# Rotated queries and keys kept in DRAM as head, frequency, half, high or low

## The chip, the cores and the metric

One core of one Trainium2 chip runs the kernel. The metric is the device time of one execution in microseconds (us), and lower is better. The kernel before takes 2559.37 us, the median of three runs (2557.65 to 2565.87).

## The reference

Two decoder layers work on 1024 tokens of width 1024, in float32. Each layer has a mixer with three groups of heads side by side, and then an MLP. Cut to what matters here:

```python
def hybrid_layer(x, ...):
    z = rms_norm(x, g_pre_mix) @ w_in
    mq, mk, mv, mo, mi, mf, sq, sk, sv, dq, dk, dv = split_columns(z)
    # mLSTM: 4 heads of 64, a causal convolution on q and k, a scan over 8 chunks of 128
    h_m = mlstm_chunkwise(...)
    # sliding window attention: 8 query heads, 2 key heads of 64, window 128, sinks
    s_q, s_k = rope(sq, pos), rope(sk, pos)
    out_s = sliding_window_gqa(s_q, s_k, s_v, sinks)
    # differential attention: 4 heads, two maps each, query and key width 32, causal
    d_q, d_k = rope(dq, pos), rope(dk, pos)
    out_d = rms_norm(differential_attention(d_q, d_k, d_v, lam), sub_g) * (1 - lam_init)
    x = x + rms_norm(concat([out_m, out_s, out_d]) @ w_out, g_post_mix)
    u = square(relu(rms_norm(x, g_pre_mlp) @ w_up))
    return x + rms_norm(u @ w_down, g_post_mlp)

def rope(x, pos):          # x: (batch, seq, heads, d)
    x1, x2 = x[..., :d // 2], x[..., d // 2:]
    return concat([x1 * cos - x2 * sin, x2 * cos + x1 * sin])
```

The rotation acts on each frequency of a head: entry p of the first half and entry p of the second half are turned together. The order in which the rows of a head lie does not matter for the scores, as long as queries and keys have the same order.

## The kernel before

Matrix products are done with each float32 operand split into a high part (rounded to the matmul's format) and a low part (the rest), so that one product becomes two or three matmuls (high by high, high by low, low by high).

A layer goes through these stages. In the first layer: the gates and values (`p_g2`), the projection of the differential queries and keys (`p_d`), the differential attention (`e_diff`), the projection of the window attention's queries and keys (`p_s`), the values and output gates of the mLSTM (`p_g1`), its queries and keys (`p_m`), the window attention together with the mLSTM, the output projection, the MLP. In the second layer `p_d` comes ahead of `p_g2`, and `p_m` ahead of `p_s`. The tile scheduler orders every engine's instructions beforehand, by priorities (`ahead(n)` raises them); each engine then runs its list in that order, and the stages named above overlap: matmuls of `p_s` (line 285) stand between those of the differential attention (lines 493, 520, 528).

A projection (`proj_tiles`) gives 128 rows by 512 tokens at a time in PSUM, for each of two halves of the sequence. For the rotated operands the columns of the weights are permuted on the host, so that one projection tile holds the first halves of several heads, 16 or 32 frequencies each, and the next tile the second halves. `rope_pair` rotates a pair of such tiles on the vector engine (DVE) into two tiles `rot`, splits each with `hi_lo`, and stores the parts to scratch tensors in DRAM. `rope_single` does the same for the keys of the window attention, where both halves lie in one tile. These stores are four for a pair of tiles and half of the sequence: two tiles, high and low each. Per layer 16 go to `d_rope` (256 KB each), 16 to `s_ropeq` (256 KB) and 8 to `s_ropek` (128 KB).

The attention stages load the rows back in the layout that the matmuls want: `diff_load` (lines 446 to 466) puts the high rows of a head's keys into 32 partitions and its high and low rows into 64 more, and the queries so that high meets low; the sum over 96 partitions is then the three products at once. `swa_load` (lines 573 to 590) does so for the window attention with 128 partitions. So these loads cannot begin before the stores have landed.

Nearly all DMA instructions, stores and loads and weights (`rw`, line 109), are issued by one engine, SyncE (SP), in one order that was fixed when the kernel was built. SP waits in front of each for whatever that transfer needs. A tile `rot` shares its buffers with other tiles (tags `e` and `at`, `ws` and `pt`), so that a buffer is free again only when its store has landed; `oo` (line 556), the last tile of a differential head, goes to `mix_d` by a store on SP too and shares the buffers `od` with `ot` (line 530).

Of the kernel before, what the change touches and what calls it, by code (L numbers as in the profile page):

```python
# [10 lines left out]
F32 = mybir.dt.float32  # L11
# [7 lines left out]
T = 1024  # L19
# [15 lines left out]
def hybrid_kernel(ctx: ExitStack, tc: tile.TileContext, x_in, w_t, w_g, w_v, w_out, w_up, w_down,  # L35
                  pb, cv, gains, g_mlp, rope_t, masks, out):
    nc = tc.nc
# [31 lines left out]
    dr = ctx.enter_context(tc.tile_pool(name="dr", bufs=2, space=bass.MemoryType.DRAM))  # L69
# [3 lines left out]
    def new(tag, shape, name, dt=F32):  # L73
        return pools[tag].tile(list(shape), dt, name=name, tag=tag)
# [7 lines left out]
    def EV(name, dt=F32, shape=(P, 512)):  # L82
        return new("ev", shape, name, dt)

    def PS(tag, name):
        return new(tag, (P, 512), name)

    def ahead(n):

        return tc.high_priority(offset=n) if n else nullcontext()  # L90
# [112 lines left out]
    for j in range(4):  # L203
        if j == 1:
            load_x(1)
        r = new("wd", (P, 2, 392), "wg0")
# [11 lines left out]
    for l in range(DEPTH):  # L218
# [22 lines left out]

        d_rope = [dr.tile([8, 2, 2, 16, T], F32, name=f"d_rope{i}") for i in range(2)]
        s_ropeq = dr.tile([8, 2, 2, 32, T], F32, name="s_ropeq")
        s_ropek = dr.tile([2, 2, 2, 32, T], F32, name="s_ropek")
        m_qk = dr.tile([4, P, T], F32, name="m_qk")
        m_v = dr.tile([T, 256], F32, name="m_v")
        m_g = dr.tile([T, 256], F32, name="m_g")
# [6 lines left out]
        def proj_tiles(*groups):  # L256


            wts = []
            for idx, _, _, _, wtag in groups:  # L260
                for i in idx:
                    if wtag == "whl":
                        w = new("whl", (P, 2, 1024), "wt", F32R)
                        hi, lo = w[:, 0], w[:, 1]
                    else:
                        hi, lo = (new(wt_, (P, 1024), "wt", F32R) for wt_ in wtag)
                    load_w(hi, lo, w_t[l, i], 512)
                    wts.append((hi, lo))
            for half in range(2):
                wi = iter(wts)  # L270
                for idx, evac, tables, rtag, _ in groups:
                    if tables is not None:
                        with ahead(1000):
                            tab = new(rtag[1], (P, 2, 512), "tab")
                            nc.sync.dma_start(tab, rope_t[tables, :, :, half * 512:(half + 1) * 512])
                    qs = []
                    for i in idx:
                        hi, lo = next(wi)
                        q = PS("mm", "pt")
                        n = 0  # L280
                        for k in range(8):
                            kc = slice(k * P, (k + 1) * P)
                            for a, b in ((hi[:, kc], hT[half][:, :, kc]), (hi[:, kc], lT[half][:, :, kc]),
                                         (lo[:, kc], hT[half][:, :, kc])):
                                nc.tensor.matmul(q, lhsT=a, rhs=b, start=n == 0, stop=n == 23)  # L285
                                n += 1
                        qs.append(q)
                        if tables is None:
                            with ahead(1000):
                                evac(i, half, q)  # L290
                    if tables is not None:
                        with ahead(1000):
                            evac(half, qs, tab, rtag[0])

        def hi_lo(r, store):

            hi = r[:, 0].bitcast(F32R)
            nc.scalar.copy(hi, r[:, 1])
            store(0)
            nc.vector.tensor_sub(r[:, 1], r[:, 1], r[:, 0])  # L300
            store(1)

        def rope_pair(d, h0, nh):

            def f(half, qs, tab, tag):
                qa, qb = qs
                c, sn = tab[:, 0], tab[:, 1]
                hs = slice(half * 512, (half + 1) * 512)
                ra, rb = (new(tag, (P, 2, 512), "rot") for _ in range(2))
                t = EV("t")  # L310
                nc.vector.tensor_mul(ra[:, 1], qa, c)
                nc.vector.tensor_mul(rb[:, 1], qa, sn)
                nc.vector.tensor_mul(t, qb, sn)
                nc.vector.tensor_sub(ra[:, 1], ra[:, 1], t)
                nc.vector.tensor_mul(t, qb, c)
                nc.vector.tensor_add(rb[:, 1], rb[:, 1], t)
                for x_, r in enumerate((ra, rb)):
                    hi_lo(r, lambda s_: nc.sync.dma_start(d[h0:h0 + nh, s_, x_, :, hs], r[:, s_]))
            return f

        def rope_single(d):

            def f(half, qs, tab, tag):
                q, = qs
                c, sn = tab[:, 0], tab[:, 1]
                hs = slice(half * 512, (half + 1) * 512)
                r = new(tag, (P, 2, 512), "rot")
                t = EV("t")
                nc.vector.tensor_mul(r[:, 1], q, c)
                nc.vector.tensor_mul(t[0:64], q[64:128], sn[64:128])  # L330
                nc.vector.tensor_mul(t[64:128], q[0:64], sn[0:64])
                nc.vector.tensor_sub(r[0:64, 1], r[0:64, 1], t[0:64])
                nc.vector.tensor_add(r[64:128, 1], r[64:128, 1], t[64:128])
                def store(s_):
                    for x_ in range(2):
                        nc.sync.dma_start(d[:, s_, x_, :, hs], r[x_ * 64:(x_ + 1) * 64, s_])
                hi_lo(r, store)
            return f

# [106 lines left out]
        def diff_load(h, hf):  # L446

            ks = []
            if hf == 0:
                k_ = new("wd", (P, 2, 512), "ks", F32R)  # L450
                src = d_rope[1][2 * h:2 * h + 2, :, :, :, 0:512].rearrange("m s x p n -> (s x p) m n")
                nc.sync.dma_start(k_[0:32].bitcast(F32), src[0:32])
                nc.sync.dma_start(k_[32:96].bitcast(F32), src)
                ks = [k_[:, m] for m in range(2)]
            else:
                for m in range(2):
                    k_ = new("wd", (P, T), "ks", F32R)
                    src = d_rope[1][2 * h + m].rearrange("s x p n -> (s x p) n")
                    nc.sync.dma_start(k_[0:32].bitcast(F32), src[0:32])
                    nc.sync.dma_start(k_[32:96].bitcast(F32), src)  # L460
                    ks.append(k_)
            q_ = new("wd", (P, 2, 512), "qs", F32R)
            src = d_rope[0][2 * h:2 * h + 2, :, :, :, hf * 512:(hf + 1) * 512].rearrange("m s x p n -> (s x p) m n")
            nc.sync.dma_start(q_[0:64].bitcast(F32), src)
            nc.sync.dma_start(q_[64:96].bitcast(F32), src[0:32])
            return ks, q_

        drd = {}
# [104 lines left out]
        def swa_load(kv, hf):  # L573
            if hf == 0:
                kk = []
                for s_ in range(2):
                    k_ = new("ws", (P, T), "kk", F32R)
                    for j in range(2):
                        nc.sync.dma_start(k_[j * 64:(j + 1) * 64].bitcast(F32),
                                          s_ropek[kv, s_].rearrange("x p n -> (x p) n"))  # L580
                    kk.append(k_)
                sop["k"] = kk
            qq = []
            for pr in range(2):
                w = new("ws", (P, 2, 512), "qq", F32R)
                h0 = kv * 4 + pr * 2
                nc.sync.dma_start(w.bitcast(F32), s_ropeq[h0:h0 + 2, :, :, :, hf * 512:(hf + 1) * 512]
                                  .rearrange("m s x p n -> (s x p) m n"))
                qq.append(w)
            sop["q"] = qq  # L590

        def swa1(kv, i):
            if i % 4 == 0:
                swa_load(kv, i // 4)
# [334 lines left out]
            acc.extend(BIG3(f"acc{i}", F32) for i in range(2))  # L929

        def p_d():
            proj_tiles(((0, 1), rope_pair(d_rope[0], 0, 8), 0, ("e", "at"), "whl"),
                       ((2, 3), rope_pair(d_rope[1], 0, 8), 1, ("e", "at"), ("wd", "ws")))

        def p_g2():
# [88 lines left out]
        for c in range(len(ffs)):  # L1024
# [30 lines left out]
            def down_mm(q, t, n, f, i):  # L1055
                for a, b in ((0, 0), (0, 1), (1, 0)):
                    nc.tensor.matmul(q, lhsT=U[f][a][:, t * P:(t + 1) * P], rhs=D[f][b][:, n * 512:(n + 1) * 512],  # L1057
                                     start=i == 0, stop=i == 3 * nf - 1)
                    i += 1
                return i  # L1060
# [43 lines left out]
            for j, (t, n) in enumerate(groups[4:]):  # L1104
                q = PS(ptag[j % 4], "pd")
                i = 0
                for f in range(nf):
                    i = down_mm(q, t, n, f, i)
# [93 lines left out]
```

## Time and profile before

| what | value |
|---|---|
| median of 3 runs | 2559.37 us |
| the profiled execution, its own time | 2563.38 us |
| its span, first to last instruction | 2561.6 us |
| TensorE matmul busy | 2397.5 us (94%) |
| VectorE busy | 1457.8 us (57%) |
| ScalarE busy | 1076.1 us (42%) |
| DMA, moved in all | 227.42 MB, mean 89 GB/s |
| chain that ended last: PE, DMA, DVE | 73%, 11%, 7% |

The span stands 1.8 us below the execution's own time, and that execution stands 4.0 us above the median of the three runs. PE is TensorE, DVE is VectorE, ACT is ScalarE, POOL is GpSimd, SP is SyncE; "SPq" marks DMA issues by SP. A row of the chain of waits has the start in us, the duration in us, and what the chain went through. A row of a table of stretches has the stretch, its length, the busy us of PE, of its weight loads, of DVE, ACT and POOL with instruction counts, the clock that TensorE was granted (1.00 is full), the mean busy share of the core's 16 DMA engines, and what they moved in GB/s. A row of the timeline of SP has start, duration, line, transfer and count; where several issues are merged, the duration includes waits between them.

### The profile page before, as it was taken

To read this page: it belongs to the slowest core of one execution; us is meant where nothing else is said; L and a number is where in the kernel's file an instruction comes from. 1 tells how busy PE (TensorE), PEld (TensorE's weight loads), DVE (VectorE), ACT (ScalarE), POOL (GpSimd) and SP (SyncE) were. 2 spreads that over 40 slices of the span, in tenths; PEclk is the share of its full clock that TensorE was granted. 3 is DMA by queue.
4 is the path that set the end of the run, shared out by engine and by line. 5 is a ranking of instruction groups with operands and counts; after the bars stand their busy time and mean duration, and the time that the engine had idled before them with its cause. 6 is when DMAs were issued, how large, how long until landed. Compare 5 with 4: busy or idle time off the path is not lost.

```text
span 2561.6 us, 32491 instructions
## 1 busy us (share of the span) xinstructions
PE 2397.5 (94%) x11556; PEld 1991.8 (78%) x11556; DVE 1457.8 (57%) x3604; ACT 1076.1 (42%) x2657; POOL 90.8 (4%) x174
## 2 busy tenths in 40 slices
PE   8888989889999999999999998878899999999998
PEld 7767867667888888888778777867678888888887
DVE  6676888775234434443675876867742344334436
ACT  4244777656313312331433645756553123213312
POOL 0000000010000000000000000000100000000000
PEclk9998999999999999999999989989999999999999
DMA  5444354333012101110442334433321112112204
GB/s 169 146 141 132 92 125 121 100 103 107 25 41 66 59 24 50 66 50 25 173 163 86 117 126 132 137 87 106 113 90 41 34 58 66 32 36 66 66 22 160
DMA packets 146002, 227.42 MB, mean 89 GB/s; under 512 B 22512, under 2 KB 60592, under 8 KB 145840
## 3 DMA queue, kind: packets, MB, share of 16 engines
q1 hardware_dynamic: 143680, 221.70, 28.1%
q10 hardware_dynamic: 2160, 3.65, 0.4%
q8 instruction: 91, 1.49, 0.2%
q14 instruction: 71, 0.58, 0.1%
HBM read 179.09 MB, written 46.20 MB: 88 GB/s over the span
## 4 chain that ended last, share of the span: by engine, by line
PE 73%; DMA 11%; DVE 7%; ACT 4%; issue 2%; POOL 1%; SPq 1%; DVEq 0%; POOLq 0%; ACTq 0%
PE pu L1012 26%; PE pd L1057 25%; PE pt L285 7%; PE po L848 2%; PE pg L356 2%; PE pn L356 2%; POOL rs L153 1%; DMA mb<-m_rows 1%; DMA qs<-d_rope 1%; PE pv L528 1%; DMA mix_d<-oo 1%; PE sp L493 1%; DMA mxl<-mix_d 1%; DMA rw<-in_w_t_dram 1%; PE ss L611 1%
## 5 line engine op out<-in xcount | busy, mean ns | idle before, releaser
L1012 PE MATMUL pu<-h2T,wu 128*128 128x512 f32 x3072 | 703.6, 390 | 0.1
L1012 PEld LDWEIGHTS pu<-h2T,wu 128*128 128x128 f32 x3072 | 577.4, 188 | 121.2 <-DVE h2T L94 1.1
L1057 PE MATMUL pd<-wdh,u 128*128 128x512 f32 x2048 | 635.2, 390 | 1.1 <-DVE acm L1068 1.1
L1057 PEld LDWEIGHTS pd<-wdh,u 128*128 128x128 f32 x2048 | 384.8, 188 | 81.1 <-DVE acm L1068 1.5
L1057 PE MATMUL pd<-wdl,u 128*128 128x512 f32 x1024 | 399.0, 390 | 0.0
L1068 DVE TENSOR_TENSOR acm<-acm,pd 128x512 f32<-128x512 f32 x224 | 153.1, 686 | 309.1 <-PE pd L1057 309.0
L1015 ACT ACTIVATE r<-pu 128x512 f32<-128x512 f32 x128 | 75.2, 588 | 537.9 <-PE pu L1012 537.9
L285 PE MATMUL pt<-hT,wt 128*128 128x512 f32 x832 | 287.2, 411 | 2.7 <-DVE lamp L228 1.5
L116 ACT ACTIVATE wu<-rw,gk 128x128 fp32r<-128x128 f32 x512 | 160.2, 390 | 184.7 <-PE pu L1012 132.3
L117 DVE SCALAR_TENSOR_TENSOR wu<-rw,gk,wu 128x128 fp32r<-128x128 f32 x512 | 154.2, 351 | 140.9 <-ACT wu L116 140.8
L1057 PEld LDWEIGHTS pd<-wdl,u 128*128 128x128 f32 x1024 | 192.6, 188 | 39.8
L1018 DVE TENSOR_TENSOR r<-r 128x512 f32<-128x512 f32 x128 | 88.4, 690 | 222.5 <-ACT u L1017 222.5
L285 PEld LDWEIGHTS pt<-hT,wt 128*128 128x128 f32 x832 | 160.5, 196 | 33.6 <-issue 2.3
L285 PE MATMUL pt<-lT,wt 128*128 128x512 f32 x416 | 170.2, 409 | 0.0
L153 POOL TENSOR_TENSOR rs<-ms,mhalf 128x1 f32<-128x1 f32 (+2 forms) x112 | 78.9, 709 | 2351.8 <-DVE ms L151 2283.2
L94 DVE TENSOR_TENSOR wdl<-rw,wdh 128x512 fp32r<-128x512 f32 x128 | 88.5, 692 | 105.1 <-ACT wdh L93 105.0
L848 PE MATMUL po<-woh,mxl 128*128 128x512 f32 x384 | 135.1, 410 | 10.4 <-DVE acc L856 7.8
L93 ACT CAST wdh<-rw 128x512 fp32r<-128x512 f32 x128 | 79.3, 620 | 129.2 <-DMA rw<-in_w_down_dram 129.2
L499 ACT ACTIVATE e<-e,nb 128x256 f32<-128x256 f32 (+7 forms) x128 | 99.4, 777 | 52.4 <-DVE nb L496 47.1
L493 PE MATMUL sp<-ks,qs 96*128 96x512 f32 (+2 forms) x192 | 74.0, 396 | 41.0 <-DMA qs<-d_rope 17.0
L356 PE MATMUL pn<-wv,hT 128*128 128x256 f32 x512 | 110.0, 296 | 0.2 <-ACT mv L707 0.2
L496 DVE CUSTOM_DVE_ANT_0 e<-sp,mdif 128x512 f32<-128x512 f32 (+3 forms) x128 | 74.5, 585 | 33.1 <-PE sp L493 24.0
(225 smaller groups left out, 3361.0 us busy)
## 6 DMA issues: line engine op xcount, KB each, us to landing
rw<-in_w_up_dram SPq DMA_DIRECT2D x128, 256.0 KB
rw<-in_w_down_dram SPq DMA_DIRECT2D x128, 256.0 KB
rw<-in_w_t_dram SPq DMA_DIRECT2D x52, 256.0 KB
tab<-in_rope_dram SPq DMA_DIRECT2D x20, 512.0 KB
xt<-in_x_dram SPq DMA_DIRECT2D x16, 512.0 KB
d_rope<-rot SPq DMA_DIRECT2D x32, 256.0 KB
s_ropeq<-rot SPq DMA_DIRECT2D x32, 256.0 KB
qq<-s_ropeq SPq DMA_DIRECT2D x16, 512.0 KB
```

The costliest lines, as they stand in the source:

```text
L94: nc.vector.tensor_sub(lo, src, hi.bitcast(F32))
L116: nc.scalar.activation(hi[:, cs], rj, AF.Copy, scale=g)
L117: nc.vector.scalar_tensor_tensor(out=lo[:, cs], in0=rj, scalar=g, in1=hi[:, cs].bitcast(F32), op0=ALU.mult, op1=ALU.subtract)
L153: nc.gpsimd.tensor_tensor(out=rs, in0=ms, in1=mhalf[:, 0:n], op=ALU.pow)
L285: nc.tensor.matmul(q, lhsT=a, rhs=b, start=n == 0, stop=n == 23)
L356: nc.tensor.matmul(q[:, 0:n], lhsT=a, rhs=b, start=i == 0, stop=i == 23)
L493: nc.tensor.matmul(sp[:, 0:w], lhsT=qs[0:96, m, (q % 4) * P:(q % 4 + 1) * P], rhs=ks[m][0:96, c0:c0 + w], start=True, stop=True)
L499: nc.scalar.activation(e[:, 0:L], e[:, 0:L], AF.Exp, bias=nb[:, nch - 1:nch], scale=-1.0, accum_out=den[:, m:m + 1])
L848: nc.tensor.matmul(q, lhsT=mx[:, a, k], rhs=wo[k][b][:, n * 512:(n + 1) * 512], start=i == 0, stop=i == 3 * nk - 1)
L1012: nc.tensor.matmul(q, lhsT=w[:, a, kc], rhs=h2[b + half][:, :, kc], start=n == 0, stop=n == 23)
L1057: nc.tensor.matmul(q, lhsT=U[f][a][:, t * P:(t + 1) * P], rhs=D[f][b][:, n * 512:(n + 1) * 512], start=i == 0, stop=i == 3 * nf - 1)
L1068: nc.vector.tensor_add(a, a, q)
```

## The change

The three scratch tensors get another order of dimensions. Before, a head's block was laid out as high or low, half (`x`), frequency, token. Now it is frequency, half, high or low, token. A store takes one half and one of high or low for all heads and all frequencies; its rows on the DRAM side are now `(h p)`, 128 rows of equal spacing (64 for `s_ropek`), where they were 8 heads of 16 rows, 4 heads of 32 rows or 2 heads of 32 rows. The spacing of the 2 KB rows of one store is 16 KB now; before it was 4 KB within a head.

The loads follow. The 64 rows of a head, now in the order frequency, half, high or low, still lie next to each other. The rows of the high parts alone are every second row now. For the differential queries the roles are turned: low comes first in memory (`low_first`), the load of 32 rows brings what is stored at place 1 (the high parts), and it is issued ahead of the load of 64 rows. For the window attention's keys each load of 64 rows goes to every second partition (`k_[j::2]`), 0, 2, 4 ... or 1, 3, 5 ..., where it went to partitions 0 to 63 or 64 to 127.

```diff
-        d_rope = [dr.tile([8, 2, 2, 16, T], F32, name=f"d_rope{i}") for i in range(2)]
-        s_ropeq = dr.tile([8, 2, 2, 32, T], F32, name="s_ropeq")
-        s_ropek = dr.tile([2, 2, 2, 32, T], F32, name="s_ropek")
+        d_rope = [dr.tile([8, 16, 2, 2, T], F32, name=f"d_rope{i}") for i in range(2)]
+        s_ropeq = dr.tile([8, 32, 2, 2, T], F32, name="s_ropeq")
+        s_ropek = dr.tile([2, 32, 2, 2, T], F32, name="s_ropek")
...
-        def rope_pair(d, h0, nh):
+        def rope_pair(d, h0, nh, low_first=False):
...
-                    hi_lo(r, lambda s_: nc.sync.dma_start(d[h0:h0 + nh, s_, x_, :, hs], r[:, s_]))
+                    hi_lo(r, lambda s_: nc.sync.dma_start(
+                        d[h0:h0 + nh, :, x_, 1 - s_ if low_first else s_, hs].rearrange("h p n -> (h p) n"), r[:, s_]))
...
-                        nc.sync.dma_start(d[:, s_, x_, :, hs], r[x_ * 64:(x_ + 1) * 64, s_])
+                        nc.sync.dma_start(d[:, :, x_, s_, hs].rearrange("h p n -> (h p) n"), r[x_ * 64:(x_ + 1) * 64, s_])
...
-                src = d_rope[1][2 * h:2 * h + 2, :, :, :, 0:512].rearrange("m s x p n -> (s x p) m n")
-                nc.sync.dma_start(k_[0:32].bitcast(F32), src[0:32])
-                nc.sync.dma_start(k_[32:96].bitcast(F32), src)
+                src = d_rope[1][2 * h:2 * h + 2, :, :, :, 0:512]
+                nc.sync.dma_start(k_[0:32].bitcast(F32), src[:, :, :, 0].rearrange("m p x n -> (p x) m n"))
+                nc.sync.dma_start(k_[32:96].bitcast(F32), src.rearrange("m p x s n -> (p x s) m n"))
...
-                    src = d_rope[1][2 * h + m].rearrange("s x p n -> (s x p) n")
-                    nc.sync.dma_start(k_[0:32].bitcast(F32), src[0:32])
-                    nc.sync.dma_start(k_[32:96].bitcast(F32), src)
+                    src = d_rope[1][2 * h + m]
+                    nc.sync.dma_start(k_[0:32].bitcast(F32), src[:, :, 0].rearrange("p x n -> (p x) n"))
+                    nc.sync.dma_start(k_[32:96].bitcast(F32), src.rearrange("p x s n -> (p x s) n"))
...
-            src = d_rope[0][2 * h:2 * h + 2, :, :, :, hf * 512:(hf + 1) * 512].rearrange("m s x p n -> (s x p) m n")
-            nc.sync.dma_start(q_[0:64].bitcast(F32), src)
-            nc.sync.dma_start(q_[64:96].bitcast(F32), src[0:32])
+            src = d_rope[0][2 * h:2 * h + 2, :, :, :, hf * 512:(hf + 1) * 512]
+            nc.sync.dma_start(q_[0:32].bitcast(F32), src[:, :, :, 1].rearrange("m p x n -> (p x) m n"))
+            nc.sync.dma_start(q_[32:96].bitcast(F32), src.rearrange("m p x s n -> (p x s) m n"))
...
-                        nc.sync.dma_start(k_[j * 64:(j + 1) * 64].bitcast(F32),
-                                          s_ropek[kv, s_].rearrange("x p n -> (x p) n"))
+                        nc.sync.dma_start(k_[j::2].bitcast(F32), s_ropek[kv, :, :, s_].rearrange("p x n -> (p x) n"))
...
-                                  .rearrange("m s x p n -> (s x p) m n"))
+                                  .rearrange("m p x s n -> (p x s) m n"))
...
-            proj_tiles(((0, 1), rope_pair(d_rope[0], 0, 8), 0, ("e", "at"), "whl"),
+            proj_tiles(((0, 1), rope_pair(d_rope[0], 0, 8, True), 0, ("e", "at"), "whl"),
```

The instructions of PE, DVE, ACT and POOL stay the same and stand in the same order. On SP the order stays too, but for the two query loads of a head, of which the smaller is now the first. Two places on SP show it. The first is in the first layer, where the keys of the window attention are stored while the differential attention runs; before:

```order
L460 DMA ks<-d_rope_191 64x1024
L464 DMA qs<-d_rope_190 64x2x512
L336 DMA s_ropek<-rot 2x32x512 x4
L465 DMA qs<-d_rope_190 32x2x512
L275 DMA tab<-in_rope_dram 128x2x512
```

and now:

```order
L462 DMA ks<-d_rope_191 64x1024
L466 DMA qs<-d_rope_190 32x2x512
L338 DMA s_ropek<-rot 64x512 x4
L467 DMA qs<-d_rope_190 64x2x512
L276 DMA tab<-in_rope_dram 128x2x512
```

The four key stores stand between the two query loads of the next head (`qs`) in both; the load behind them is now the one of 64 rows (256 KB), and it was the one of 32 rows (128 KB). The second place is in the second layer, where queries of the window attention are stored; before:

```order
L318 DMA s_ropeq<-rot 4x32x512 x3
L109 DMA rw<-in_w_t_dram 128x512 x2
L464 DMA qs<-d_rope_11178 64x2x512
L465 DMA qs<-d_rope_11178 32x2x512
L459 DMA ks<-d_rope_11179 32x1024
L460 DMA ks<-d_rope_11179 64x1024
L558 DMA mix_d<-oo 64x256
```

and now:

```order
L319 DMA s_ropeq<-rot 128x512 x3
L109 DMA rw<-in_w_t_dram 128x512 x2
L466 DMA qs<-d_rope_11178 32x2x512
L467 DMA qs<-d_rope_11178 64x2x512
L461 DMA ks<-d_rope_11179 32x1024
L462 DMA ks<-d_rope_11179 64x1024
L560 DMA mix_d<-oo 64x256
```

Here nothing but the order within the pair of query loads has moved; the stores ahead of them have another shape on the DRAM side.

## The prediction

> **What bounds the kernel now.** I read the chain of waits first, then tables of stretches around each place where it runs through a DMA in the attention part, then the timeline of SP there. The change can act only where rotated tiles are stored and loaded back, in the attention part of each layer. There the chain has long DMA pieces:
>
> ```profile
> 98.99 6.41 DMA rw<-in_w_t_dram
> 126.39 11.16 DMA qs<-d_rope
> 161.59 7.86 DMA ks<-d_rope
> 194.71 3.72 issue
> 221.08 10.12 DMA mix_d<-oo
> ...
> 1341.87 5.75 DMA rw<-in_w_g_dram
> 1461.40 12.51 DMA qs<-d_rope
> 1500.91 8.68 DMA qs<-d_rope
> 1532.20 9.55 DMA mix_d<-oo
> 1562.28 8.30 DMA mix_d<-oo
> 1572.41 3.00 DMA ks<-d_rope
> ```
>
> A load of 256 KB takes 3.00 us when little stands ahead of it (last row); the others, of 64 to 256 KB, take 5.75 to 12.51. What stands ahead is seen in the table of stretches (the last two columns are the share of 16 DMA engines and GB/s):
>
> ```profile
> 133.00:139.00 6.00, 1.31 (x4) 1.25 (x5) 0.51 (x1) 0.00 (x0) 0.00 (x0) 0.70 0.13 51
> 160.00:161.00 1.00, 1.00 (x9) 0.91 (x8) 1.00 (x3) 0.09 (x1) 0.00 (x0) 1.00 0.25 96
> 112.00:116.00 4.00, 3.90 (x18) 2.92 (x17) 1.73 (x7) 1.91 (x6) 0.00 (x0) 1.00 0.52 186
> 1405.50:1406.00 0.50, 0.50 (x3) 0.38 (x2) 0.50 (x4) 0.50 (x3) 0.00 (x0) 1.00 1.03 393
> ```
>
> Behind key stores (2 heads outermost) the share is 0.13, two engines of 16, for six microseconds on end; behind the window queries' stores (4 heads) 0.25, four engines; behind the differential stores (8 heads) 0.52, eight. About 24 to 25 GB/s an engine each time. The last stretch lies behind one store of 256 KB with 128 rows (`m_qk`, alone in the queue): all engines, 393 GB/s. So the stores crowd onto as many engines as their outermost dimension has rows, and every later transfer that has a share of its bytes on those engines waits behind them.
>
> [...]
>
> SP suffers too:
>
> ```profile
> 1404.59 0.34 SPq L691 DMA_DIRECT2D m_qk<-yc  x1
> ...
> 1458.46 2.90 SPq L336 DMA_DIRECT2D s_ropek<-rot  x4
> ...
> 1467.47 8.00 SPq L336 DMA_DIRECT2D s_ropek<-rot  x4
> ```
>
> Four key stores hold SP for 2.90 us, and while earlier ones still drain, 8.00.
>
> **The change part by part.** *Stores.* Four key stores are 4 x 128 KB = 0.52 MB: 10.3 us at 51 GB/s, 1.3 at 393, 9.0 less. Four query stores of the window attention, 1.05 MB: 10.9 us at 96 GB/s, 2.7 at 393, 8.2 less. Four differential stores: 5.6 us at 186 GB/s, 2.7 after, 2.9 less. These times matter only where someone waits. Ten gaps of PE lie there, each followed by a stretch with a reduced granted clock (column before the last two):
>
> ```profile
> 102.50:107.60 5.10, 0.00 (x1) 0.00 (x0) 1.53 (x5) 0.62 (x1) 0.00 (x0) 0.71 0.32 109
> 107.60:112.00 4.40, 4.38 (x12) 3.60 (x13) 4.23 (x12) 2.12 (x7) 0.00 (x0) 0.56 0.41 111
> 132.00:137.70 5.70, 0.19 (x2) 0.05 (x1) 0.69 (x1) 0.17 (x1) 0.00 (x0) 0.79 0.13 51
> 137.70:142.00 4.30, 4.30 (x13) 3.72 (x14) 2.40 (x8) 1.59 (x7) 0.00 (x0) 0.50 0.20 63
> 164.60:169.50 4.90, 0.00 (x0) 0.03 (x1) 2.15 (x6) 1.50 (x3) 0.00 (x0) 1.00 0.49 155
> 169.50:174.00 4.50, 4.50 (x14) 3.73 (x15) 2.98 (x5) 1.72 (x3) 0.00 (x0) 0.62 0.26 87
> 194.70:198.40 3.70, 0.01 (x1) 0.00 (x1) 2.20 (x6) 2.09 (x9) 0.89 (x2) 0.78 0.61 223
> 198.40:204.00 5.60, 5.57 (x15) 4.41 (x16) 1.78 (x9) 0.05 (x1) 0.00 (x0) 0.53 0.64 209
> 228.00:235.50 7.50, 1.42 (x6) 1.04 (x5) 1.35 (x5) 2.72 (x9) 0.89 (x2) 0.69 0.80 197
> 235.50:238.00 2.50, 2.44 (x11) 2.47 (x12) 1.78 (x5) 0.49 (x2) 0.00 (x0) 0.50 0.33 128
> 1345.00:1348.60 3.60, 0.00 (x0) 0.00 (x0) 0.41 (x1) 0.94 (x2) 0.00 (x0) 0.79 0.25 87
> 1348.60:1353.00 4.40, 3.81 (x11) 3.40 (x12) 4.33 (x9) 1.14 (x2) 0.00 (x0) 0.50 0.45 103
> 1467.60:1474.00 6.40, 0.00 (x0) 0.00 (x0) 0.66 (x2) 0.92 (x4) 0.89 (x2) 0.68 0.45 158
> 1474.00:1480.00 6.00, 5.96 (x15) 4.72 (x16) 4.10 (x13) 0.00 (x0) 0.00 (x0) 0.50 0.32 107
> 1505.60:1509.80 4.20, 0.00 (x0) 0.00 (x0) 0.98 (x2) 1.56 (x5) 0.00 (x0) 0.73 0.19 69
> 1509.80:1515.00 5.20, 5.17 (x15) 4.15 (x16) 3.62 (x9) 2.71 (x5) 0.89 (x2) 0.56 0.50 144
> 1538.00:1542.80 4.80, 0.96 (x6) 0.49 (x4) 0.98 (x5) 1.34 (x6) 0.00 (x0) 0.88 0.57 199
> 1542.80:1548.00 5.20, 5.18 (x14) 4.21 (x15) 2.31 (x9) 2.31 (x7) 0.89 (x2) 0.50 0.31 80
> 1570.50:1576.00 5.50, 1.96 (x14) 1.59 (x13) 1.56 (x6) 2.46 (x8) 0.89 (x2) 0.98 0.84 191
> 1576.00:1579.00 3.00, 3.00 (x16) 2.94 (x15) 1.97 (x7) 0.62 (x3) 0.00 (x0) 0.50 0.00 0
> ```
>
> Idle time of PE in the gaps: 5.1 + 5.5 + 4.9 + 3.7 + 6.1 in the first layer, 3.6 + 6.4 + 4.2 + 3.8 + 3.5 in the second, 46.8 us. Behind each, length times missing clock: 1.9 + 2.2 + 1.7 + 2.6 + 1.3 and 2.2 + 3.0 + 2.3 + 2.6 + 1.5, 21.3 us. All of it together, 68 us, is the most that the gaps can give.
>
> Gap by gap: the second and the seventh wait for a query load behind key stores; 9.0 us less is more than the gap, and 126.39 + 3.0 or 1461.40 + 3.0 lies ahead of where PE ran dry (132.0, 1467.6). I take gap and clock: 7.7 and 9.4. The third and the eighth wait behind window query stores; 161.59 + 3.0 and 1500.91 + 3.0 are no later than 164.6 and 1505.6: 6.6 and 6.5. The first and the sixth wait for weights behind differential stores: 2.9 us each, clock not counted since a gap remains. In the other four the share is 0.57 to 0.84, so bandwidth for loads is needed there anyway, or the chain names no cause ("issue"); between nothing and all I take half of gap and clock: 3.2, 3.7, 3.2, 2.5. Sum: 24.1 + 24.5 = 48.6 us.
>
> *What comes back.* When DMA is early, DVE is late next. It did 1.5 + 0.7 + 2.2 + 2.2 + 1.4 and 0.4 + 0.7 + 1.0 + 1.0 + 1.6 = 12.5 us inside the gaps, and right behind them it has little room:
>
> ```profile
> 140.00:164.00 24.00, 23.68 (x115) 19.07 (x115) 21.36 (x56) 12.90 (x32) 0.90 (x2) 0.95 0.50 157
> ```
>
> 89% of that stretch. So of the work done in the gaps I charge the part of the gaps that goes, 48.6 of 68: 8.9 us. Net 39.7.
>
> *Loads.* Same bytes in rows of the same length. The second query load brings 128 KB more behind the key stores, 0.3 us at 393 GB/s, with 2.6 us to spare at 132.0: nothing; without that cover, 0.3 a head. Keys to every second partition is a form that the trace does not have. Its nearest row is the same load as now:
>
> ```profile
> 1688.57 9.37 DMA kk<-s_ropek
> ```
>
> Four groups of such loads run per execution. If they took twice as long, at most 4 x 9.4 = 37 us; if shorter, the same bound below nothing. I take nothing, since rows, bytes and the number of rows per load are the same.
>
> *Issue.* A store of 128 rows may cost SP 0.34 us (`m_qk`) where four key stores now cost 0.7 each at best; SP's long holds end. I count nothing: those holds are the same time as the waits above.
>
> **The rivals.** *DVE and ACT take over, the gain is small.* For it: 89% above. Then only the four gaps behind 2 and 4 engines give their idle time, 5.5 + 6.4 + 4.9 + 4.2 = 21.0, less DVE's work in them, 4.5: 16.5 us, 2543 against the median; with two of the four refilled, 8 us, 2551. Against it: in the gaps DVE and ACT mostly stand still with PE, so all are delayed alike.
>
> *No change that can be told.* The loads are late anyway: in 228.0 to 235.5 and in 1570.5 to 1576.0 the engines are 0.80 and 0.84 busy, and spread stores put bytes on engines that had been free for loads. That all ten gaps are such is against the 0.13 of the second. That the stores do not spread although they are now 128 rows (the change not doing what it says) is against the 393 GB/s of `m_qk`. Within 7.7 us of 2559.
>
> *Slower: rows 16 KB apart.* One store now writes 2 KB in every 16 KB, and if DRAM takes such a pattern badly, all 16 engines stand in a slow write and everything queues behind it. Now a layer's stores take 4 x 5.6 + 4 x 10.9 + 2 x 10.3 = 86.6 us for 9.4 MB, 109 GB/s; below that the change loses. At 51 GB/s it would be 185 us, 98 more per layer; as 68 of 173 us are on the path now, 0.39 of 197 is 77 us: 2636. For it, no store of the trace has this spacing; against it, `m_qk` writes 2 KB in every 4 KB at full rate.
>
> [...]
>
> **How the numbers follow.** Profiled execution 2563.4 - 39.7 = 2523.7; it stands 4.0 above the median, so 2519.6 for a median. The first case (16 to 68 us won, 2491 to 2543) has 0.72, more than 68 won 0.02, DVE taking over with 8 to 16 won 0.10, no change 0.10, slower 0.06. The range goes from all gaps and clocks gone, 2491, to just past the four gaps' bound, 2547, which leaves out the lower half of the small gains, no change and slower. A difference under 0.3%, 7.7 us, cannot be told from none: faster 0.84, same 0.10, slower 0.06.
>
> **What would show it.** In the profile after: stretches with a share of 0.13, 0.25 or 0.5 in the store batches give way to short ones near 1.0; the query load behind the key stores is under 4.5 us in the chain or gone from it; the gaps at the second, third, seventh and eighth place go, with the half clock behind them; four key stores hold SP under 3 us each time; DVE's share in these stages rises. It would be wrong if the gaps stay with a load or DVE named in place of the store, if stores show a high share at low GB/s (the slower rival), or if the key loads to every second partition turn up longer than 9.4 us.

## The result, and the profile after

The changed kernel takes 2483.06 us (median of 4 runs, 2480.93 to 2487.86) against 2559.03 of the kernel before: ratio 0.9701, 95% interval 0.9678 to 0.9723. That is 76 us won, where 40 were forecast. The direction and the mechanism hold; the time lies outside the range, which ended at 2491. The profiled execution has a span of 2486.1 us, 75.5 less than before.

The page of the changed kernel gives the chain of waits by engine; DMA had 11% of it before:

```profile
span 2486.1 us, 32491 instructions
PE 78%; DVE 8%; DMA 5%; ACT 4%; issue 2%; POOL 2%; SPq 0%; POOLq 0%; DVEq 0%; ACTq 0%
```

In the changed kernel the places of the former gaps read as follows, in the table of stretches (columns as before). The first four rows lie where the first, second, third and fifth gap lay in the first layer, the last three where the seventh and the eighth lay in the second:

```profile
102.00:107.00 5.00, 5.00 (x25) 4.03 (x24) 4.73 (x13) 2.31 (x7) 0.00 (x0) 1.00 0.33 107
125.00:130.00 5.00, 5.00 (x29) 4.01 (x28) 4.13 (x13) 2.37 (x8) 0.00 (x0) 1.00 0.75 206
150.00:155.00 5.00, 5.00 (x24) 4.16 (x23) 5.00 (x12) 3.42 (x6) 0.00 (x0) 1.00 0.78 261
201.50:207.00 5.50, 5.47 (x46) 5.23 (x45) 3.96 (x15) 3.52 (x11) 0.89 (x2) 1.00 0.40 131
...
1424.50:1430.00 5.50, 5.47 (x28) 4.05 (x27) 5.09 (x16) 2.44 (x7) 0.89 (x2) 1.00 0.85 267
1430.00:1436.00 6.00, 6.00 (x35) 5.02 (x34) 5.56 (x18) 3.92 (x13) 0.00 (x0) 1.00 0.05 18
1453.00:1458.00 5.00, 5.00 (x24) 4.15 (x24) 4.68 (x12) 2.48 (x4) 0.89 (x2) 1.00 0.54 163
```

PE is busy throughout these rows and the granted clock is 1.00; at the other four places it is the same. DVE is 83 to 100% busy in six of the seven rows, and it does not hold PE up. In the view of who waits for whom, from 55 to 210 us, these are all waits of PE that are left (name, what ended the wait, us in total, times, the longest); in the second layer, from 1300 to 1560, the longest is 0.7 us:

```profile
PE trd L522 <- DVE on L549: 0.6, 1, 0.6
PE sp L495 <- DVE nb L498: 0.5, 1, 0.5
PE nat L540 <- DVE on L549: 0.4, 1, 0.4
PE pt L286 <- DVE rot L313: 0.2, 1, 0.2
PE trd L522 <- ACT oo L559: 0.2, 1, 0.2
```

No DMA is left among the long pieces of the chain in either stretch. The stores land early (DMA issues of the changed kernel; the last number is the median time from issue to landing), and SP is no longer held by four key stores (timeline of SP, second layer):

```profile
d_rope<-rot SPq DMA_DIRECT2D x32, 256.0 KB, 3.2
s_ropeq<-rot SPq DMA_DIRECT2D x32, 256.0 KB, 2.7
s_ropek<-rot SPq DMA_DIRECT2D x16, 128.0 KB, 2.3
```

```profile
1415.37 2.79 SPq L338 DMA_DIRECT2D s_ropek<-rot  x4
...
1423.83 2.39 SPq L338 DMA_DIRECT2D s_ropek<-rot  x4
```

The second group held SP for 8.00 us before, and does so for 2.39 now.

Since PE's instructions are the same in the same order, every matmul of one trace can be set against the same matmul of the other. The table has, at matmuls around the ten gaps, how much earlier each runs than in the kernel before (us), for the changed kernel and for four experiments told below; worked out from the start times in the traces:

```
start before   changed   none spread   only d_rope   only s_ropek   only s_ropeq
    95.6        -1.6        -0.5           1.1           -1.5           -1.6
   118.5         6.2        -0.5           8.7           -1.7           -1.5
   142.1        13.7        -1.1           7.8            5.8           -2.4
   180.0        20.4        -0.5           7.8            5.7            4.3
   215.1        26.5        -0.2           8.0            7.2           10.4
   260.0        35.6         1.4           9.6            8.0           19.5
  1300.8        34.6         2.9           8.5           10.5           18.3
  1362.1        43.1         2.9          17.1           11.2           17.9
  1490.0        52.6         4.8          17.7           20.8           18.2
  1520.1        59.2         5.5          17.6           21.3           24.8
  1556.1        65.4         8.7          17.5           24.2           31.0
  1580.1        70.7         9.7          18.3           25.9           36.2
  1630.3        70.5         9.7          18.3           25.9           36.1
  1860.0        76.0         7.5          19.2           50.0           29.7
```

The gain comes in ten steps at the ten gaps: 7.7, 7.6, 6.7, 6.1, 9.1 in the first layer, 8.5, 9.6, 6.6, 6.2, 5.2 in the second, 73.3 us together (from unrounded differences). Ahead of the first the changed kernel is 1.6 us behind, and behind the last it wins another 4.8. Between the steps the difference hardly moves; in the whole MLP it stands still (34.4 from 600 to 1200).

Each trace is one execution, and that limits how finely the columns can be read: `none spread` rises to 9.7 although no store is spread, by up to 3 us at a gap, but its trace is 4 us under the median of its kernel and that of the kernel before 4 us above its own. A step of 2 or 3 us is not taken as an effect here.

### The profile page after: what moved, and what is told of

The parts are those of the page before. It is cut to its first block, busy times and chain, and to the rows that moved or that the text cites. A ratio compares the mean times of both kernels' runs of the same rounds, so it can differ in the third digit from the quotient of the medians.

```text
span 2486.1 us, 32491 instructions
## 1 busy us (share of the span) xinstructions
PE 2380.3 (96%) x11556; PEld 1977.1 (80%) x11556; DVE 1456.5 (59%) x3604; ACT 1074.4 (43%) x2657; POOL 91.3 (4%) x174
## 4 chain that ended last, share of the span: by engine, by line
PE 78%; DVE 8%; DMA 5%; ACT 4%; issue 2%; POOL 2%; SPq 0%; POOLq 0%; DVEq 0%; ACTq 0%
PE pu L1013 26%; PE pd L1058 26%; PE pt L286 9%; PE po L849 3%; PE pn L358 3%; PE pg L358 2%; POOL rs L153 2%; DMA mb<-m_rows 2%; PE pv L530 2%; PE sp L495 1%; PE trd L522 1%; DMA mxl<-mix_d 1%; PE ss L612 1%; ACT junk L159 1%; PE pvs L646 1%
## 5 line engine op out<-in xcount | busy, mean ns | idle before, releaser
L286 PE MATMUL pt<-hT,wt 128*128 128x512 f32 x832 | 279.5, 401 | 2.0 <-DVE lamp L228 1.5
L1058 PEld LDWEIGHTS pd<-wdl,u 128*128 128x128 f32 x1024 | 192.5, 188 | 39.9
L286 PEld LDWEIGHTS pt<-hT,wt 128*128 128x128 f32 x832 | 155.5, 190 | 31.0 <-issue 1.9
L849 PEld LDWEIGHTS po<-woh,mxl 128*128 128x128 f32 x384 | 73.3, 194 | 22.9 <-DVE acc L857 7.9
L1020 DVE TENSOR_TENSOR u<-r,u 128x512 fp32r<-128x512 f32 x128 | 88.5, 691 | 4.0
```

Of the source, the lines that this page charges most:

```text
L849: nc.tensor.matmul(q, lhsT=mx[:, a, k], rhs=wo[k][b][:, n * 512:(n + 1) * 512], start=i == 0, stop=i == 3 * nk - 1)
L1020: nc.vector.tensor_sub(us[1][:, hs], r, us[0][:, hs].bitcast(F32))
```

## The experiments

**Which stores, and stores or layout.** The changed kernel reorders rows and spreads stores at once. A gap of one unused row group behind each head in DRAM keeps the new order, the spacing of 16 KB and every load, but the rows of a store no longer have one spacing, so that it is 8 x 16, 4 x 32 or 2 x 32 rows again. This can be done for each family of stores by itself. The edit for all three (`none spread`) follows; in the other three it is two of these lines. In all four kernels the stores name heads and frequencies as two dimensions, and where no gap lies between the heads they run spread all the same: with only the key tensor left without gaps, its stores move 205 GB/s at a share of 0.87 (127 to 128 in that trace), where the share was 0.13 before; the other two families won the steps of the changed kernel that way (table).

```diff
-        d_rope = [dr.tile([8, 16, 2, 2, T], F32, name=f"d_rope{i}") for i in range(2)]
-        s_ropeq = dr.tile([8, 32, 2, 2, T], F32, name="s_ropeq")
-        s_ropek = dr.tile([2, 32, 2, 2, T], F32, name="s_ropek")
+        d_rope = [dr.tile([8, 17, 2, 2, T], F32, name=f"d_rope{i}")[:, 0:16] for i in range(2)]
+        s_ropeq = dr.tile([8, 33, 2, 2, T], F32, name="s_ropeq")[:, 0:32]
+        s_ropek = dr.tile([2, 33, 2, 2, T], F32, name="s_ropek")[:, 0:32]
```

All three gaps, no store spread:

> The new layout with 17 or 33 row groups kept for a head instead of 16 or 32, so that the rows of a store are 8 x 16, 4 x 32 or 2 x 32 again and cannot be taken as one row count; rows, spacing of 16 KB, and every load as in the changed kernel. Theory A (only the number of engines that a store runs on matters): the gain goes, 2559 within 8 us, and shares of 0.13, 0.25 and 0.5 are back behind the stores. Rival B (the order of rows in DRAM, or the keys to every second partition, brings the gain): near the changed kernel, 2483 to 2500.

Measured: 2560.14 us, ratio 0.9985 (0.9972 to 0.9999). The gain goes with the spread, and with it the signs come back. From this kernel the chain, the table of stretches and the timeline of SP:

```profile
126.90 12.14 DMA qs<-d_rope
```

```profile
134.00:136.00 2.00, 0.00 (x0) 0.00 (x0) 0.00 (x0) 0.00 (x0) 0.00 (x0) 0.94 0.13 51
```

```profile
131.19 8.71 SPq L338 DMA_DIRECT2D s_ropek<-rot  x4
```

Two of 16 engines at 51 GB/s, PE idle, SP held for 8.71 us: as in the kernel before, although rows, spacing and loads are the new ones. Rival B falls.

Only the differential stores spread:

> Only the differential stores run on 16 engines (8 before); the window attention's stay at 4 and 2. Theory A, by how much earlier the matmuls at the first and the sixth gap run in the changed kernel (8.6 and 8.5 us): about 2542. By the prediction's price for these gaps (2.9 us each): 2553. Rival C (one queue, so that what is won at one family of stores is waited for at the next): within 8 us of 2559.

Measured: 2549.6 us, ratio 0.9938 (0.9918 to 0.9959), 14 us under the kernel before as timed beside it (2563.62). In the table its column rises by 7.7 at the first gap and 8.5 at the sixth, the amounts of the changed kernel, and by no more than 1.7 at any other. The two prices stood for 17 and 6 us; the 14 us of the whole kernel lie between them, and the steps decide for the larger one.

Only the key stores spread:

> Only the window attention's key stores run on 16 engines (2 before). Theory A, by the shift at the second and the seventh gap (7.6 and 9.5 us; the prediction had 7.7 and 9.4): about 2542. Rival C: within 8 us of 2559, since the query stores on 4 engines come right behind.

Measured: 2517.57 us, ratio 0.9817 (0.9798 to 0.9835), 46 us. In the attention part the steps are the expected ones, 7.6 at the second gap and 9.5 at the seventh. But from 1630 to 1860, where no rotated tile is stored, this kernel wins another 24 us that none of the others has. That was not expected and is followed up below.

Only the window queries' stores spread:

> Only the window attention's query stores run on 16 engines (4 before). Theory A, by the shift at the other six gaps (6.7, 6.0, 9.1, 6.6, 6.3, 5.2 us): 40 us won, about 2519, and the three gains of single families add up to that of the changed kernel, 74 to 76. By the prediction's halves for four of these gaps: 26 us, 2533. Rival C: the single gains add up to much less than 74.

Measured: 2528.8 us, ratio 0.9859 (0.9839 to 0.988), 35 us. Steps at the third, fourth and fifth and at the eighth, ninth and tenth gap, 6.7, 6.1, 9.1, 6.6, 6.2 and 5.2: 39.9 us. The time falls 5 us short of them, since between 1580 and 1860 this kernel loses 6.5 (table), for a cause that stays open. So the fourth, fifth, ninth and tenth gap were all stores on 4 engines, and went whole.

The three families' steps, 16.2 + 17.1 + 39.9, make 73.2, the changed kernel's 73.3, gap by gap: nothing won at one family is paid back at another. By the times of the whole kernels it is 14, 46 and 35, together 95, and 71 without the 24 us that have another cause. Rival C falls.

**A dose.** The differential tensors with a gap in the middle only, so that these stores have 2 x 64 rows and run on 2 engines; the window attention's stores stay spread, and the loads read the same rows:

```diff
-        d_rope = [dr.tile([8, 16, 2, 2, T], F32, name=f"d_rope{i}") for i in range(2)]
+        d_rope = [dr.tile([2, 65, 2, 2, T], F32, name=f"d_rope{i}")[:, 0:64] for i in range(2)]
...
+                        (d[h0:h0 + nh] if nh == 4 else d)[:, :, x_, 1 - s_ if low_first else s_, hs], r[:, s_]))
```

> The changed kernel, with a gap between the first four and the last four heads of the differential queries and keys, so that these stores have 2 rows of 64 outermost: 2 engines, where they had 8 before and 16 in the changed kernel; all else as changed. Theory A (a store of 256 KB takes 5.1 us on 2 engines, four of them 20.6 us where 16 engines take 2.7): much slower than the changed kernel, about 100 us, between 2540 and 2630, though the window attention's stores are spread. Rival B (layout and loads matter): 2483.

Measured: 2583.42 us (2 runs), ratio to the kernel before 1.0101 (1.0076 to 1.0127), 100 us over the changed kernel. Set against the changed kernel's matmuls, it falls back by 64 us at the differential stores of the first layer and by 61 in the second, of which 24 come back in the second layer's window attention and mLSTM stage (more on that below). Its chain and its table of stretches:

```profile
106.93 13.95 DMA rw<-in_w_t_dram
133.61 13.99 DMA rw<-in_w_t_dram
156.31 18.06 DMA d_rope<-rot
```

```profile
110.00:120.00 10.00, 0.00 (x0) 0.00 (x0) 0.00 (x0) 0.00 (x0) 0.00 (x0) 0.51 0.24 86
```

A weight load of 256 KB takes 14 us behind stores on 2 engines, and all four compute engines stand still for 10 us. The share of 0.24 is a mean: it is 0.13 to 0.14, two engines, at 49 to 53 GB/s for each microsecond from 107 to 112. The price followed the engines: 125 us for 2 instead of 16, 16 for 8 instead of 16.

**The keys to every second partition.**

```diff
-                        nc.sync.dma_start(k_[j::2].bitcast(F32), s_ropek[kv, :, :, s_].rearrange("p x n -> (p x) n"))
+                        nc.sync.dma_start(k_[j * 64:(j + 1) * 64].bitcast(F32), s_ropek[kv, :, :, s_].rearrange("p x n -> (p x) n"))
...
-                nc.sync.dma_start(w.bitcast(F32), s_ropeq[h0:h0 + 2, :, :, :, hf * 512:(hf + 1) * 512]
-                                  .rearrange("m p x s n -> (p x s) m n"))
+                for s_ in range(2):
+                    nc.sync.dma_start(w[s_ * 64:(s_ + 1) * 64].bitcast(F32), s_ropeq[h0:h0 + 2, :, :, s_, hf * 512:(hf + 1) * 512]
+                                      .rearrange("m p x n -> (p x) m n"))
```

> The changed kernel, with the window attention's keys loaded to partitions 0 to 63 and 64 to 127 again, and its queries in two loads of 64 rows, high and low, in place of one of 128. Prediction's step (keys to every second partition cost or bring nothing): 2483 within 8 us, with 16 more issues on SP. Rival: the spread partitions are part of the gain, 10 us or more slower than the changed kernel.

Measured: 2491.08 us, ratio to the kernel before 0.9741 (0.9725 to 0.9757), 8 us over the changed kernel. That is just outside the first expectation and short of the rival's 10; set side by side, the two ratios to the kernel before make it 10. So it is not decided, and the 16 more issues are in it. In the traces the loss is 4 us, and all of it lies behind 1741 of the kernel before; the ten steps are there. The median landing of a key load is 4.1 us here and 3.9 in the changed kernel, which gives no sign that the form of the key load matters.

**The 24 us in a stage without these stores.** In the kernel with only the key stores spread, two scratch tensors are larger, so every DRAM tensor allocated behind them lies elsewhere. To part place from the rest, the changed kernel got the same sizes with the unused rows at the end, heads side by side:

```diff
-        d_rope = [dr.tile([8, 16, 2, 2, T], F32, name=f"d_rope{i}") for i in range(2)]
-        s_ropeq = dr.tile([8, 32, 2, 2, T], F32, name="s_ropeq")
+        d_rope = [dr.tile([136, 2, 2, T], F32, name=f"d_rope{i}")[0:128].rearrange("(h p) x s n -> h p x s n", h=8) for i in range(2)]
+        s_ropeq = dr.tile([264, 2, 2, T], F32, name="s_ropeq")[0:256].rearrange("(h p) x s n -> h p x s n", h=8)
```

> The changed kernel, with each scratch tensor of the differential queries and keys and of the window attention's queries as large as in the kernel where only the key stores were spread (136 and 264 row groups), but the unused rows at the end, so that heads lie side by side and all stores run on 16 engines; every later DRAM tensor lies where it lay there. That kernel won 22 us in the second layer's window attention and mLSTM stage, where no rotated tile is stored, by the matmul-by-matmul comparison. Theory P (it is the place in DRAM of the tensors behind, read there in 512 B pieces): 2483 - 20, about 2463. Rival T (it is how the transfers of that stage fall in time): 2483 within 8 us, or anything that does not repeat the 22.

Measured: 2460.62 us, ratio 0.9622 (0.9601 to 0.9642), 22 us under the changed kernel; set against its matmuls, 23 us come between 1560 and 1741. It is the place. Not every move does it: the dose kernel, whose differential tensors are a little larger too, wins 24 us more than the changed kernel in this stage, but the kernels with no stores, only the differential and only the window queries' stores spread, which move the tensors by other amounts, win nothing there (table, 1630.3 and 1860.0). The changed kernel's own tensors are as large as before the change, so its 76 us have nothing of this.

Among what is read there in small pieces are the mLSTM's gate rows, `m_rows`: for each chunk four rows of 512 B, the same ones to all 128 partitions. (`m_qk` is read in pieces of 512 B as well, and `m_v` of 256 B.) A kernel that keeps the rows of a chunk together reads the same bytes in pieces of 2 KB and 1 KB:

```diff
-        m_rows = dr.tile([32, 2, P], F32, name="m_rows")
+        m_rows = dr.tile([2, NT, 4, P], F32, name="m_rows")
...
-            nc.sync.dma_start(m_rows, rows)
+            nc.sync.dma_start(m_rows[0].rearrange("c h n -> h c n"), rows[:, 0])
+            for g in range(2):
+                nc.sync.dma_start(m_rows[1, :, g::2].rearrange("c b n -> b c n"), rows[g * 16:(g + 1) * 16, 1])
...
-            mr = m_rows.rearrange("(h c) a n -> c a h n", c=NT)
-            nc.sync.dma_start(rb, mr[c, 0].partition_broadcast(P))
+            nc.sync.dma_start(rb, m_rows[0, c].partition_broadcast(P))
...
-                    nc.sync.dma_start(ai[b * 64:(b + 1) * 64], mr2[c, 1, b].partition_broadcast(64))
+                    nc.sync.dma_start(ai[b * 64:(b + 1) * 64], m_rows[1, c, 2 * b:2 * b + 2].partition_broadcast(64))
```

> The changed kernel, with the mLSTM's gate rows kept in DRAM so that what one chunk reads lies together: loads in pieces of 2 KB and 1 KB in place of 512 B, the same bytes. In the changed kernel's profile these loads land after 7.8 us in the median, and ScalarE waits 32.4 us for them. Theory: pieces of 512 B are what makes them slow, several us off most of these waits, 2455 to 2475. Rival: they are late because they stand behind others on SP, 2483 within 8 us.

Measured: 2421.62 us, ratio to the kernel before 0.9473 (0.9454 to 0.9493), 61 us under the changed kernel: more than expected. Against the changed kernel's matmuls 35 us come in the first layer, where moving the tensors brought 2, and 29 in the second. The issues of the large gate loads with their median landing, and who waits for them, first in the changed kernel:

```profile
mb<-m_rows SPq DMA_DIRECT2D x16, 256.0 KB, 8.8
...
ACT mb L756 <- DMA mb<-m_rows: 32.4, 7, 7.5
```

then with the rows together:

```profile
mb<-m_rows SPq DMA_DIRECT2D x16, 256.0 KB, 3.7
...
ACT mb L756 <- DMA mb<-m_rows: 5.5, 3, 2.3
```

and with the tensors moved, rows as before:

```profile
mb<-m_rows SPq DMA_DIRECT2D x16, 256.0 KB, 7.5
```

The same 256 KB land after 8.8 us in the changed kernel, 7.5 with the tensors moved and 3.7 with the rows together. The 64 KB loads of `m_v` went the same way in these three: 8.1, 6.0 and 3.4 us.

Small pieces alone were not what was slow. In the changed kernel the loads of `m_qk` have the same form, four pieces of 512 B for each of 128 partitions, but every partition reads bytes of its own:

```profile
mb<-m_qk SPq DMA_DIRECT2D x16, 256.0 KB, 3.5
```

They land after 3.5 us where the gate rows take 8.8.

Both steps together, rows together and tensors moved:

> The kernel with gate rows in pieces of 2 KB and 1 KB (2422), and the unused rows behind the scratch tensors of the kernel that came to 2461. Theory P1 (the place in DRAM matters only to the reads in pieces of 512 B, the gate rows above all): no further gain, 2422 within 8 us. Rival P2 (it matters to the mLSTM's other loads): another 20 us, about 2400.

Measured: 2421.82 us, ratio 0.9469 (0.9452 to 0.9487). No further gain: with the gate rows in pieces of 2 KB and 1 KB the two places differ by 0.2 us, 2421.62 and 2421.82 (P1).

And the rows together in the kernel before, with its old layout:

> The kernel before, old layout and stores on 8, 4 and 2 engines, with only the gate rows in pieces of 2 KB and 1 KB. Theory: that gain lies in another stage and adds to the change's, 61 us again, about 2498 to 2502. Rival: part of it needs the earlier stores (SP's queue), less than 45 us, over 2513.

Measured: 2491.63 us, ratio 0.9739 (0.9724 to 0.9755), 66 us, a little more than expected. The two gains add: 76 and 61 from one side, 66 and 70 from the other. The kernel with the change and the gate rows together, 2422 us, beats both kernels of this study.

## Why the prediction was right in kind and wrong in size

- *What bounds.* Right for the stores measured: with 2, 4 and 8 rows outermost they ran at shares of 0.13, 0.25 and 0.52, as many engines of 16, and later transfers waited behind them. The kernel that takes the spread away alone shows it (0.13, 51 GB/s and the gain gone), and so does the dose (2 rows, 0.13 to 0.14, a weight load of 14 us). Eight engines at 186 GB/s are 23 an engine, under the 24 to 25 named. SP's long holds went too, 8.00 to 2.39 us.
- *Key stores of 64 rows on 16 engines.* The rows beside the prediction have none; that they would move at the 393 GB/s of 128 rows, 1.3 us for four, was the author's estimate, and no run shows it. In the changed kernel they stand at a share of 0.88 to 0.90, but at 203 to 209 GB/s (rows in the last section).
- *Behind two and four engines, the whole gap and its clock.* Right within 0.2 us: forecast 7.7, 6.6, 9.4 and 6.5 us for the second, third, seventh and eighth gap, measured 7.6, 6.7, 9.6 and 6.6.
- *Differential stores, "2.9 us each, clock not counted since a gap remains".* Wrong: 7.7 and 8.5. The price was one batch of four stores, 5.6 less 2.7 us, and so much the landing did give: the weights that the first gap waits for take 3.7 us from their issue at 97.79, and took 6.4; those of the sixth take 2.4, and took 5.75. What it left out is that these weights are also issued earlier, by 2.8 and 3.2 us when set against the same matmuls. At the first gap the delay had begun one weight load before: ScalarE had waited 7.67 us for that one, until 92.87, and now waits for PE there. So ScalarE has the weights of the first gap 5.5 us earlier, not 2.9: 105.42 less 101.55 (rows below), and 1.6 that the changed kernel was behind in that trace (table). No gap remains (stretch 102 to 107), so the half clock behind it goes as well. 10.4 us of the miss.
  ACT's timeline, of the kernel before and of the changed one:

```profile
105.42 0.62 ACT L93 CAST wt<-rw 128x512 fp32r<-128x512 f32 x1 [7.89 <-DMA rw<-in_w_t_dram]
```

```profile
101.55 0.62 ACT L93 CAST wt<-rw 128x512 fp32r<-128x512 f32 x1 [4.89 <-DMA rw<-in_w_t_dram]
```

- *Half of the four gaps with a share over 0.5.* Wrong: 6.1, 9.1, 6.2 and 5.2 against 3.2, 3.7, 3.2 and 2.5. A mean share of 0.57 to 0.84 was read as bandwidth that loads need anyway. The kernel with only the window queries' stores spread wins all four whole, so it was the stores' own backlog on four engines. 14.0 us of the miss. The fifth gave 1.7 more than its idle time and clock (7.4): the half clock behind it lasted to about 241, and the prediction's row ends at 238.
- *"What comes back", 8.9 us for DVE.* Wrong: nothing came back. DVE reached 83 to 100% at most places where the gaps had been, and PE's waits there are 0.7 us at the most. The steps add up gap by gap, which a bound by DVE would not let them do.
- *Together:* 39.7 + 10.4 + 14.0 + 8.9 is 73.0, and the four exact gaps add 0.3: the 73.3 of the steps. The 68 us, held to be the most that the gaps can give, were too low, since the rows cut some of them short: besides the fifth, PE stood still at the sixth from 1343.9, and the row begins at 1345.
- *Loads at nothing.* Right within what was measured: order, spacing and key loads together, with the places moved too, are 3.5 us of gain in the kernel with no store spread. The old form of the key loads, with 16 more issues, costs 8 to 10 us, of which the share of the form is open.
- *A sign of being wrong that did come.* Four key loads of the second layer land after 9.7 to 10.0 us, over the 9.4 that was named. The chain does not go through them, and their form does not explain it: in the kernel with the tensors moved the same form lands after 7.1 us at the most.
- *The slower rival.* It did not come. Behind the query stores of the window attention, 2 KB in every 16 KB, the engines move 343 GB/s; the prediction's price was 393, from `m_qk`. From the changed kernel's table of stretches:

```profile
139.50:142.50 3.00, 3.00 (x14) 2.45 (x13) 2.96 (x8) 2.70 (x6) 0.00 (x0) 1.00 0.97 343
```

## What to carry to other kernels

Look in the trace for stretches where the DMA share stands at an even fraction while something waits. Here 0.13, 0.25 and 0.52 stood behind stores with 2, 4 and 8 rows outermost, and the cost was paid by what was queued behind them: query loads of 11.16 and 12.51 us behind the key stores, weight loads of 14 us in the dose kernel. In a scratch tensor try an order of dimensions in which the rows of a store have one spacing and make one large outermost dimension: here such stores of 128 rows stood at a share of 0.97 and 343 GB/s, those of 64 rows at 0.88 to 0.90 and 203 to 209 GB/s, and a pad between heads undid it (0.13 and 51 GB/s, 2560.14 us). When a gap is caused by a backlog, count also what made the late transfer start late, not only the batch it stands behind, and do not halve the price of a gap because the mean share in it is high: at shares of 0.57 to 0.84 four gaps gave 26.6 us here, where half of them had been put at 12.6.

## What the runs showed of the hardware that was not expected

Key stores of 64 partitions now keep 0.88 to 0.90 of the 16 engines busy, but each of these moves less; from the changed kernel's table of stretches:

```profile
119.00:120.00 1.00, 1.00 (x6) 0.84 (x5) 0.97 (x3) 0.25 (x1) 0.00 (x0) 1.00 0.88 203
120.00:121.00 1.00, 1.00 (x6) 0.81 (x5) 1.00 (x4) 0.00 (x0) 0.00 (x0) 1.00 0.90 209
```

A share of 0.9 with 203 to 209 GB/s is 14 GB/s an engine, where the stores of 128 partitions at the same spacing had 22 (343 at 0.97, above). The 393 GB/s of the prediction's price came from a store of 128 partitions and did not hold for these: at 206 GB/s four of them take 2.5 us instead of 1.3. That leaves 7.8 of the 9.0 us that the prediction had for them, still more than the gaps of 5.5 and 6.4 us that it was set against. Why 64 partitions moved less an engine stays open: no run here varies their number alone.

Moving tensors in DRAM, and that alone, changed the time by 22 us: four rows of 512 B, 8 KB apart, read for all 128 partitions, landed after 8.8 us in the median, and after 7.5 with the tensors moved. With the rows of a chunk in one piece the place made 0.2 us (2421.62 and 2421.82). Neither piece size nor repeated reading was enough by itself here: `m_qk`, in pieces of 512 B but with bytes of its own for each partition, lands after 3.5 us, and the rows together, which all partitions still read, after 3.7. Whether it takes small pieces and repeated reading together, or the spacing of the rows, stays open, since the edit to the gate rows changed piece size and spacing at once; so does why one place is slower than another.
